# Hybrid decoder trunk: the instruction order made by the scheduler's timeline simulation instead of its core simulation

## The chip, the cores and the metric

The kernel runs on one core of a Trainium2 chip. The metric is the device time of one execution in microseconds (us), lower is better. The program is straight-line code: no loop is left at run time, and each engine carries out one fixed list of instructions.

## The reference

Four post-norm layers on a sequence of 1024 tokens with 1024 channels, all in float32. Layer i uses the token mixer i mod 3, so the order is short convolution, S5 state space, RWKV-7, short convolution.

```python
for i in range(DEPTH):
    kind, j = i % N_MIXERS, i // N_MIXERS
    if kind == 0:
        y = short_conv_mixer(x, conv_w_in[j], conv_k[j], conv_w_out[j])
    elif kind == 1:
        y = s5_mixer(x, ssm_w_in[j], ...)
    else:
        y = rwkv7_mixer(x, rwkv_mu[j], rwkv_w_rkvz[j], ...)
    r = DN_ALPHA * x + y
    r = r + (p[i] @ ple_proj[i]) * jax.nn.sigmoid(r @ ple_gate[i])
    x = layer_norm(r, ln_g[i], ln_b[i])
```

The convolution mixer has one 1024 x 4096 product, a convolution of width 3, gates and a 1024 x 1024 product. The S5 mixer has a 1024 x 2048 product, a diagonal complex scan and two 1024 x 1024 products. The RWKV mixer has four 1024 x 1024 products (r, k, v, z), two small low-rank products, a recurrence over the tokens with a 64 x 64 state in each of 16 heads, and a 1024 x 1024 product:

```python
def _rwkv_step(state, inp):
    r_t, w_t, k_t, v_t, kk_t, a_t = inp
    sa = jnp.einsum("bhvk,bhk->bhv", state, -kk_t)
    state = (state * w_t[:, :, None, :] + sa[..., None] * (kk_t * a_t)[:, :, None, :]
             + v_t[..., None] * k_t[:, :, None, :])
    out = jnp.einsum("bhvk,bhk->bhv", state, r_t)
    return state, out
```

## The kernel before

**Tiling.** Activations lie with channels on the 128 partitions: 8 blocks of channels (m = 0..7), and tokens in two halves of 512 (h = 0, 1). Every large product works with operands split into a high and a low part. `mm3` makes one 128 x 512 piece of a product with 24 matmuls of 512 columns: for each of 8 blocks of the contraction high times high (L308), high times low (L309) and low times high (L310). In what follows "a product" is such a piece of 24.

**Weights.** `wload` fetches one block of weights of 512 KB (L282, a DMA issued by SyncE, SP), casts it to its high part on ScalarE (`wh`, L285) and makes the low part on VectorE (`wl`, L286). Each of the three tiles has three buffers. `weight_order` lists the blocks in the order of use, and `wprep` starts the load two blocks ahead of use (`AHEAD = 2`).

**Background work.** Work that runs beside the products is written as Python generators. `pull` takes their next piece at fixed places between the products, by lists of small counts at the top of the S5 part (`CP`, `GP`, `UP`, `GR`, `IP`, `TP` and others). This sets the order in which instructions are traced. In conv layer 0 the tables of S5 are made that way, in the S5 layer the scan blocks, in the gate stages the layer norm of the half before (`ln_gen`).

**The RWKV layer.** For each half it computes z for the 8 blocks (with the low-rank parts), then v, then k and r block by block. A pair (m, h) is called a unit. For each unit `use_k` and `use_r` prepare the operands of the recurrence from the two products of k and r, `prep` makes the 64 x 64 score blocks, `tsolve` inverts unit triangular blocks on VectorE, `join` puts them together, and `seq` carries the state through 8 chunks of 64 tokens. One step of `seq`:

```python
nc.tensor.matmul(p1, R.ra[:, c, :], st, start=False, stop=False, skip_group_check=True)   # L1818
SC.copy(uv[rb, :], p1[rb, :])                                                          # L1819
p2 = sq("p2")
last = nc.tensor.matmul(p2[:, 0:P], R.kbt[c // 4][:, c % 4, :], uv, start=True, stop=True)  # L1822
for hd in range(2):
    V.scalar_tensor_tensor(st[cs, cs], st[cs, cs], R.pc[cs, c:c + 1], p2[cs, cs], ...)  # L1825
```

After the 8 steps come the output matmuls (L1832, 32 small ones), a group norm (L1846 and after), a scaling on GpSimd (L1853), a transposition on TensorE (`otp`, L1860) and a store. In `prep`, GpSimd scales `kb` (L1692), which TensorE then transposes (`kbtp`, L1697). The state goes to memory at the end of a unit of the first half (`dST`, L1837), and is fetched at the start of the same block in the second. At the turn from the first half to the second the layer reloads `x` of the second half from memory and builds the shifted operands of z from it (`xs3`).

**What sets the order.** The kernel names the engine of each operation, but not its place in the engine's list. The framework's scheduler makes the lists when the `TileContext` closes: it steps through a simulation of the core, and whenever an engine is free it gives it, out of the instructions that are ready, the one of the highest priority. Priority is the traced order, moved forward by `high_priority(offset=...)` for `tsolve` and `seq` (300) and `prep` and `join` (600). A few `issue_after` blocks forbid some moves. Buffers are handed out along the way. In the end the lists hold semaphore waits in place of the simulated times, so that on the chip each engine takes its list in order and waits at its head.

## Time and profile before

| what | value |
|---|---|
| median of 3 runs | 2874.41 us (2870.41 to 2875.98) |
| profiled execution | 2874.98 us, span 2873.3 us |
| instructions | 40597 |
| mean granted TensorE clock | 0.963 |
| busy share of TensorE (PE), its weight loads (PEld) | 95%, 75% |
| busy share of VectorE (DVE), ScalarE (ACT), GpSimd (POOL) | 66%, 39%, 22% |
| DMA | 312.67 MB, mean 109 GB/s |
| RWKV layer, from about 1150 to 2190 us | 1040 us |

The profile is one execution on the chip. Busy times are given for each engine; records of pipelined matmuls overlap, so a row of one matmul can read 0.40 us while the next starts 0.23 us later. In a table of windows each row is a stretch of the span. In a list of waits the row "A <- B" says that engine and instruction A stood idle until B ended, with the total, the number of times and the longest. L-numbers are lines of the kernel.

### The profile page before, as it was taken

The numbers are of one execution on the slowest core, as the hardware profiler recorded it, in microseconds if no ns is written. First come the engines' busy times: TensorE is split into PE (matmuls) and PEld (weight loads), VectorE is DVE, ScalarE is ACT, GpSimd is POOL, SyncE is SP. The second block draws the span as 40 slices with busy tenths as digits, with TensorE's granted clock in tenths as the row PEclk, the third lists the DMA queues.
The fourth block names the chain that finished last, engine by engine and source line by source line (L and its number), as shares of the span: only waits on it lengthen the run. The fifth ranks groups of instructions, "written<-read, shape, count | busy, mean of one in ns | idle before, by whom it ended". The sixth has DMA issues, their size and how long they took to land.

```text
span 2873.3 us, 40597 instructions
## 1 busy us (share of the span) xinstructions
PE 2722.6 (95%) x15131; PEld 2163.6 (75%) x15131; DVE 1886.0 (66%) x3428; ACT 1121.9 (39%) x2147; POOL 635.8 (22%) x690
## 2 busy tenths in 40 slices
PE   8999999999999999999888799898889999999998
PEld 6877788878877887577666577666667778888887
DVE  6787765477657347878788676887848473333654
ACT  3333322242144223655556465565534231112322
POOL 1243423221207033104333101333232210000000
PEclk9999999999999999999997799997899999999999
DMA  5333322358783333463222254222334332112320
GB/s 166 98 95 96 94 77 62 88 152 225 209 247 124 103 92 119 144 214 96 73 81 89 69 182 141 74 86 83 110 92 143 104 91 59 44 46 64 118 66 37
DMA packets 449749, 312.67 MB, mean 109 GB/s; under 512 B 48360, under 2 KB 393744, under 8 KB 449552
## 3 DMA queue, kind: packets, MB, share of 16 engines
q1 hardware_dynamic: 449552, 310.08, 36.0%
q8 instruction: 119, 1.95, 0.3%
q14 instruction: 78, 0.64, 0.1%
HBM read 240.28 MB, written 69.21 MB: 108 GB/s over the span
## 4 chain that ended last, share of the span: by engine, by line
PE 73%; DVE 14%; ACT 4%; issue 3%; POOL 2%; DMA 2%; SPq 0%; DVEq 0%; POOLq 0%; ACTq 0%
PE op L309 3%; PE op L308 3%; PE op L310 3%; PE gp L310 3%; PE zp L308 3%; PE gp L309 3%; PE zp L309 3%; PE zp L310 3%; PE gp L308 3%; PE sp L308 3%; PE sp L309 3%; PE sp L310 3%; DVE tv L1739 2%; PE hp L308 2%; PE hp L309 2%
## 5 line engine op out<-in xcount | busy, mean ns | idle before, releaser
L286 DVE TENSOR_TENSOR wl<-wraw,wh 128x1024 fp32r<-128x1024 f32 x283 | 365.9, 1294 | 311.5 <-ACT wh L285 303.5
L285 ACT CAST wh<-wraw 128x1024 fp32r<-128x1024 f32 x283 | 296.9, 1050 | 695.5 <-PE gp L309 191.8
L608 POOL TENSOR_TENSOR ln_s<-ln_s,rp 128x512 f32<-128x512 f32 x42 | 60.1, 1430 | 209.8 <-DVE rp L604 209.8
L1825 DVE SCALAR_TENSOR_TENSOR state<-state,pc,p 64x64 f32<-64x64 f32 x256 | 71.0, 277 | 50.1 <-PE p L1822 45.6
L1739 DVE TENSOR_TENSOR tv<-ti,mi 128x128 f32<-128x128 f32 (+3 forms) x128 | 97.1, 759 | 2.4
L1818 PE MATMUL p<-state,ra 128*128 128x128 f32 x256 | 65.7, 344 | 27.3 <-DVE state L1825 25.2
L1819 ACT COPY uv<-p 64x128 f32<-64x128 f32 x128 | 33.2, 259 | 138.8 <-PE p L1818 138.1
L1818 PEld LDWEIGHTS p<-state,ra 128*128 128x128 f32 x256 | 46.3, 219 | 52.7 <-DVE state L1825 42.1
L1673 PEld LDWEIGHTS s<-ra,kb 64*128 64x128 f32 x512 | 64.2, 212 | 20.4 <-ACT scr L1679 6.5
L1673 PE MATMUL s<-ra,kb 64*128 64x128 f32 x512 | 74.7, 314 | 4.4 <-ACT scr L1679 2.1
L1822 PE MATMUL p<-uv,kbt 128*128 128x128 f32 x256 | 67.7, 351 | 10.4 <-ACT uv L1819 10.3
L310 PE MATMUL gp<-r_0h,wl 128*128 128x512 f32 x192 | 76.9, 400 | 0.0
L308 PE MATMUL zp<-x_0h,wh 128*128 128x512 f32 x192 | 76.7, 400 | 0.0
L309 PE MATMUL gp<-r_0l,wh 128*128 128x512 f32 x192 | 76.7, 399 | 0.0
L308 PE MATMUL gp<-r_0h,wh 128*128 128x512 f32 x192 | 76.5, 398 | 0.0
L308 PE MATMUL gp<-r_1h,wh 128*128 128x512 f32 x192 | 76.4, 398 | 0.0
L310 PE MATMUL gp<-r_1h,wl 128*128 128x512 f32 x192 | 76.0, 396 | 0.1
L623 POOL TENSOR_TENSOR rp<-r_0h,r_0l 128x512 f32<-128x512 f32 x24 | 37.4, 1589 | 174.9 <-PE op L309 174.9
L308 PE MATMUL zp<-x_1h,wh 128*128 128x512 f32 x192 | 75.9, 396 | 0.0
L310 PE MATMUL zp<-x_1h,wl 128*128 128x512 f32 x192 | 75.8, 395 | 0.0
L309 PE MATMUL zp<-x_1l,wh 128*128 128x512 f32 x192 | 75.7, 394 | 0.0
L310 PE MATMUL zp<-x_0h,wl 128*128 128x512 f32 x192 | 75.7, 394 | 0.0
(740 smaller groups left out, 8437.6 us busy)
## 6 DMA issues: line engine op xcount, KB each, us to landing
wraw<-in_conv_w_in_dram SPq DMA_DIRECT2D x80, 512.0 KB
wraw<-in_rwkv_w_rkvz_dram SPq DMA_DIRECT2D x64, 512.0 KB
wraw<-in_ple_gate_dram SPq DMA_DIRECT2D x56, 512.0 KB
wraw<-in_conv_w_out_dram SPq DMA_DIRECT2D x24, 512.0 KB
wraw<-in_ssm_w_in_dram SPq DMA_DIRECT2D x21, 512.0 KB
xt<-xd SPq DMA_DIRECT2D x32, 256.0 KB
wraw<-in_rwkv_w_out_dram SPq DMA_DIRECT2D x16, 512.0 KB
wraw<-in_ple_proj_dram SPq DMA_DIRECT2D x14, 512.0 KB
```

The source lines that it names most:

```text
L285: nc.scalar.copy(wh, raw)
L286: nc.vector.tensor_tensor(wl, raw, f32(wh[:]), ALU.subtract)
L308: nc.tensor.matmul(ps, lh, xh, start=(k == 0), stop=False)
L309: nc.tensor.matmul(ps, lh, xl, start=False, stop=False)
L310: nc.tensor.matmul(ps, ll, xh, start=False, stop=(k == kt - 1))
L608: nc.gpsimd.tensor_tensor(s, s, rs, ALU.add)
L623: (eng or nc.gpsimd).tensor_tensor(rs, f32(rh[:]), f32(rl[:]), ALU.add)
L1673: nc.tensor.matmul(pss[hd][:, c * P:(c + 1) * P], kb[rows, 2 * c + w, :], ra[rows, 2 * c + w, :], start=True, stop=True)
L1739: V.tensor_tensor(tv, ti[:, b:8, 4 * b:4 * b + 4].unsqueeze(2).to_broadcast([P, n, c, 4]), mi[:, 4 * b:4 * b + 4, 0:c].rearrange("p q c -> ...
L1818: nc.tensor.matmul(p1, R.ra[:, c, :], st, start=False, stop=False, skip_group_check=True)
L1822: last = nc.tensor.matmul(p2[:, 0:P], R.kbt[c // 4][:, c % 4, :], uv, start=True, stop=True)
L1825: V.scalar_tensor_tensor(st[cs, cs], st[cs, cs], R.pc[cs, c:c + 1], p2[cs, cs], ALU.mult, ALU.add)
```

## The change

The scheduler steps through another simulation, the framework's timeline simulation. Both have costs for each instruction; they come from different models, in which engines, queues, transfers and semaphores are kept differently. The traced program, its priorities, its engines, its tiles and their buffer counts stay as they are.

```diff
-    with tile.TileContext(nc) as tc:
+    with tile.TileContext(nc, schedule_with_timeline_sim=True) as tc:
         body(tc, aps, out)
```

## The prediction

> **What bounds the kernel now.** I read the busy times first, then the clock, then the table of windows by layer, and last the matmuls and waits of the one layer that is left. Busy time on the page, and the clock from the view of the cores:

> ```profile
> PE 2722.6 (95%) x15131; PEld 2163.6 (75%) x15131; DVE 1886.0 (66%) x3428; ACT 1121.9 (39%) x2147; POOL 635.8 (22%) x690
> ...
> PE 73%; DVE 14%; ACT 4%; issue 3%; POOL 2%; DMA 2%; SPq 0%; DVEq 0%; POOLq 0%; ACTq 0%
> ```

> ```profile
> core 0: 2873.3 us, clock 0.963
> ```

> TensorE is busy for 95% of the span and carries 73% of the chain that ended last. An order cannot remove a matmul. It can only remove idle time of TensorE, 2873.3 - 2722.6 = 150.7 us, and time at a low clock. The windows (columns: length, busy time of PE, PEld, DVE, ACT and POOL with their counts, granted clock, DMA share, GB/s) say where both lie: before, in and after the RWKV layer.

> ```profile
> 0.00:1150.00 1150.00, 1120.84 (x5283) 904.37 (x5283) 753.66 (x1277) 369.37 (x539) 313.67 (x373) 1.00 0.44 128
> 1150.00:2190.00 1040.00, 932.58 (x6869) 713.99 (x6870) 796.99 (x1613) 570.44 (x1326) 265.46 (x264) 0.91 0.36 112
> 2190.00:2874.00 684.00, 669.22 (x2981) 545.25 (x2979) 335.38 (x540) 182.12 (x283) 56.70 (x54) 0.99 0.24 72
> ```

> Outside the RWKV layer TensorE idles 29.2 + 14.8 = 44 us in 1834 us, at a clock of 0.99 to 1.00. Inside it idles 1040 - 932.6 = 107.4 us, the clock is 0.91, and VectorE is busy for 797 us of 1040. So the order matters there.

> **What the change does there.** It adds no instruction, removes none and gives no engine other work. What moves is the place of each instruction in its engine's stream, and each engine takes its stream in that order. Within RWKV I follow one step of the recurrence, written in `seq`: a matmul of the state (L1818), a copy on ScalarE (L1819), a second matmul (L1822), two state updates on VectorE (L1825). There are 8 steps in each of 16 units (8 channel blocks, two halves), 128 in all. TensorE's stream in one step, with products of z from the turn between the halves beside it (start, duration, instruction):

> ```profile
> 1579.03 0.40 PE L1818 MATMUL p<-state,ra 128*128 128x128 f32 x2
> 1579.18 0.48 PE L310 MATMUL sp<-xs3h,wl 128*128 128x512 f32 x1
> 1579.50 0.40 PE L309 MATMUL sp<-xs3l,wh 128*128 128x512 f32 x1
> 1579.78 0.49 PE L1822 MATMUL p<-uv,kbt 128*128 128x128 f32 x2
> 1580.02 0.48 PE L310 MATMUL sp<-xs3h,wl 128*128 128x512 f32 x1
> 1580.33 0.39 PE L308 MATMUL sp<-xs3h,wh 128*128 128x512 f32 x1
> 1580.56 0.40 PE L309 MATMUL sp<-xs3l,wh 128*128 128x512 f32 x1
> 1580.79 0.39 PE L310 MATMUL sp<-xs3h,wl 128*128 128x512 f32 x1
> 1581.02 0.47 PE L1818 MATMUL p<-state,ra 128*128 128x128 f32 x2
> ```

> The step takes 1581.02 - 1579.03 = 1.99 us. While the chain is on ScalarE and VectorE, the order in place runs six large matmuls, which start 0.23 us apart (1580.33, 1580.56, 1580.79). Eight steps hold 48 of them, and 48 are two whole products of 24: as much as a unit has in its k and r stretch. What the order does is to lay these products into the gaps of the chain.

> The second measure is the time from unit to unit, by the last matmuls of each (L1832). First, last and the extreme pairs of the twelve ends that I use, six of each half of the sequence:

> ```profile
> 1420.57 1.15 PE L1832 MATMUL p<-uv,scr 128*64 128x64 f32 x32
> ...
> 1463.11 1.15 PE L1832 MATMUL p<-uv,scr 128*64 128x64 f32 x32
> ...
> 1509.00 1.15 PE L1832 MATMUL p<-uv,scr 128*64 128x64 f32 x32
> ...
> 1628.51 1.76 PE L1832 MATMUL p<-uv,scr 128*64 128x64 f32 x28
> ...
> 1851.64 1.15 PE L1832 MATMUL p<-uv,scr 128*64 128x64 f32 x32
> ...
> 1890.42 1.15 PE L1832 MATMUL p<-uv,scr 128*64 128x64 f32 x32
> ...
> 1927.03 1.15 PE L1832 MATMUL p<-uv,scr 128*64 128x64 f32 x32
> ...
> 2047.93 1.15 PE L1832 MATMUL p<-uv,scr 128*64 128x64 f32 x32
> ```

> The mean period is (1628.51 - 1420.57) / 5 = 41.6 us in the first half and (2047.93 - 1851.64) / 5 = 39.3 us in the second, 40.4 us over both. The longest is 1509.00 - 1463.11 = 45.9 us, the shortest 1927.03 - 1890.42 = 36.6 us. The recurrence work of a unit is the same each time. The spread, 3.8 us below the mean and 5.5 us above, is mostly what different orders of like work have cost in this kernel, and it bounds the change from both sides: 13 such periods (seven in each half, less the last, which runs out without products beside it) give 13 x -3.8 = -49 us and 13 x 5.5 = +71 us.

> **What an order can win.** The waits of TensorE in the layer (us in total, times, longest), then one of VectorE:

> ```profile
> PE p L1818 <- DVE state L1825: 25.2, 28, 2.8
> PE otp L1860 <- POOL o L1853: 14.1, 10, 6.8
> PE kbtp L1697 <- POOL kb L1692: 12.1, 11, 2.8
> PE p L1822 <- ACT uv L1819: 10.3, 24, 1.0
> ```

> ```profile
> DVE state L1825 <- PE p L1822: 45.6, 46, 2.9
> ```

> In each the head of a stream stood waiting, and what was behind it stood too. TensorE's four rows sum to 61.7 us. A simulation that foresees these latencies better puts other work in front. But VectorE, at 77% of the layer, needs those 45.6 us less than TensorE needs the chain: where a stall goes, the next thing late is the state update behind a weight split or a solve.

> **What an order can lose.** The gaps hold 16 x 48 x 0.23 = 177 us of products. An order that puts a unit's products in one block ahead of its chain leaves the gaps empty and pays them again in full. So the room is 61.7 us one way and 177 us the other. That asymmetry is why I put the forecast on the slower side, half way from the mean period to the longest: 13 x 2.7 = +35 us.

> **The other streams.** On SP every weight load (L282) stands in line with the stores of the recurrence:

> ```profile
> SPq L282 <- DVE state L1825: 50.9, 8, 14.9
> ```

> Eight loads stood behind a state up to 14.9 us. They cost nothing now because weights are fetched two blocks ahead (`AHEAD = 2`), which is 2 x 24 x 0.23 = 11 us of products. With that cover gone each would cost at most 14.9 - 11 = 4 us, 32 us for eight; I take nothing, since no weight row is among TensorE's largest waits, and leave it inside the range. GpSimd and ScalarE (265 and 570 us of 1040) have room; a GpSimd operation taken later shows up as the `otp` and `kbtp` rows above, 26 us, and at worst doubles them, which the +71 covers. Outside RWKV I take zero: TensorE has large products ready nearly all the time. Bounds there: -44 us, if all its idle time went, and +44 us, if it doubled, at the hand-overs between layers.

> **The sum.** The profiled execution took 2874.98 us, 1.7 around its span of 2873.3, and stands 0.6 above the median of the three runs (2874.41). 2874.98 + 35 = 2910 us.

> **The clock, and a rule.** Two stretches of 10 us show what small matmuls alone do:

> ```profile
> 1530.00:1540.00 10.00, 7.67 (x100) 5.92 (x104) 7.26 (x20) 2.64 (x8) 0.61 (x2) 0.50 0.55 173
> 2000.00:2010.00 10.00, 7.93 (x87) 6.23 (x83) 4.95 (x13) 3.65 (x8) 0.61 (x2) 0.50 0.01 3
> ```

> TensorE is busy for 77% and 79% there, so it cannot have idled more than 2.33 us at once, and yet the granted clock is 0.50. By these rows, an order that spreads large products into such stretches would lift the clock. All that it could give is 0.09 x 932.6 = 84 us. [...]

> **The rivals.**
> - Faster through better foresight: the new order fills the waits above and the units move half way to the shortest, 13 x -1.9 = -25 us: 2850 us. For it: 61.7 us of waits at the head of the stream, 46 waits of VectorE of 1 us each. Against: the six matmuls of a step already fill it. It decides once more than 35 of the 61.7 us are filled and the products stay in the gaps.
> - Faster through the clock as well: 25 us and half of the 84 us, -67 us: 2808 us. It needs products at the turn from the first half to the second, where they first need `x` reloaded.
> - Much slower: the scheduler picks TensorE's next instructions earlier than they can run, so that ready products of 24 go ahead of a chain step that is not ready yet. Half of a unit's products leave the gaps: 177 / 2 = +88 us, 2963 us; all of them +177 us, 3052 us. It decides against me once more than a fifth leave (35 of 177). Against it: later units have fewer ready products, so the block shrinks.
> - No difference: both simulations pick the same order where TensorE is the limit, or the flag does nothing. Then 2875 us. Against: the choice depends on time at every step, and one early difference shifts all that follows.

> **How the numbers follow.** Chances: longer units 0.37, much slower 0.14, better foresight 0.29, with the clock 0.07, no difference 0.13. So slower is 0.51, faster 0.36, and within 0.2% (5.7 us, about what three runs from 2870.41 to 2875.98 can tell apart) 0.13. The likeliest case by itself runs from 2881 to 2946 us. The range over the cases is 2822 to 2990 us: it holds the foresight case down to the shortest period (-49 us) and a little of the clock, and the blocked case up to 65% of the 177 us. About 0.07 is left out below and 0.08 above.

> **What would show it.** Right: nearly the same instruction counts, the windows outside RWKV within 10 us of now, the RWKV layer some 35 us longer, units 43 us apart instead of 40.4, more waits of L1818 for the state, TensorE's busy time about the same. Wrong towards faster: the four waits fall below 30 us and units come at 38 us. Wrong towards much slower: runs of 24 large matmuls with no L1818 between, and then chain steps with fewer than six. Wrong in place: if conv or S5 changes by over 20 us, the assumption that ready products cover everything outside RWKV has failed.

## Result: 9.3% slower

| | before | after |
|---|---|---|
| median of 4 runs each, one chip | 2875.19 us (2870.41 to 2881.53) | 3142.77 us (3135.47 to 3146.55) |
| ratio, 95% interval | | 1.0926 (1.0894 to 1.0958) |
| profiled span | 2873.3 us | 3144.8 us |
| TensorE busy / idle in the span | 2722.6 / 150.7 us | 2882.2 / 262.6 us |

The 271.5 us between the spans are two terms: TensorE idles 111.9 us longer, and the same 15131 matmul records occupy it 159.6 us longer. The second term is mostly the clock: 175 us of TensorE's busy time lay at half clock before and 478 us lie there after, and half of the 302 us between them is 151. First the busy times on the page and the mean granted clock of the kernel after, then its windows, cut at the same stages as the 1150 and 2190 us of before (columns as there):

```profile
PE 2882.2 (92%) x15131; PEld 2320.3 (74%) x15131; DVE 1908.2 (61%) x3428; ACT 1122.5 (36%) x2149; POOL 636.2 (20%) x690
```

```profile
core 0: 3144.8 us, clock 0.904
```

```profile
0.00:1175.00 1175.00, 1131.03 (x5283) 916.27 (x5283) 757.51 (x1271) 362.41 (x534) 317.74 (x369) 0.98 0.43 125
1175.00:2461.00 1286.00, 1087.08 (x6908) 863.61 (x6909) 816.15 (x1620) 579.91 (x1335) 262.11 (x270) 0.79 0.29 91
2461.00:3144.00 683.00, 664.04 (x2941) 540.38 (x2939) 334.48 (x538) 180.14 (x282) 56.31 (x54) 0.99 0.24 72
```

The RWKV layer grew from 1040 to 1286 us: 199 - 107 = 92 us of idle time and 1087.1 - 932.6 = 154.5 us of longer busy time. A granted clock of 0.79, made of stretches at 1.0 and at 0.5, means (1 - 0.79) / 0.5 x 1286 = 540 us at half clock; before it was (1 - 0.91) / 0.5 x 1040 = 187 us. The part ahead of it grew by 25 us. The part behind it took as long as before, but with 40 fewer matmul records in it (2941 against 2981), so some 9 us of the layer's growth are work that the new order put ahead of the cut.

Inside the layer, the last matmuls of the units (first and sixth of the first half; first, fifth and sixth of the second):

```profile
1471.98 1.98 PE L1832 MATMUL p<-uv,scr 128*64 128x64 f32 x32
...
1746.94 1.98 PE L1832 MATMUL p<-uv,scr 128*64 128x64 f32 x32
...
2046.21 1.98 PE L1832 MATMUL p<-uv,scr 128*64 128x64 f32 x32
...
2240.36 1.98 PE L1832 MATMUL p<-uv,scr 128*64 128x64 f32 x32
...
2322.45 1.15 PE L1832 MATMUL p<-uv,scr 128*64 128x64 f32 x32
```

A unit takes 55.0 us in the first half and 55.2 us in the second, where it took 41.6 and 39.3 (41.4 for the same five of the first half). The second mean is not of like work: the last of its five periods, 82.1 us, holds 198 large matmuls (almost all of the output product `op`) where it held 25 before. The four ahead of it take 48.5 us each, where they took 38.7. Part of a unit of the first half in TensorE's stream (start, duration, instruction, and in brackets the idle time before it and what ended it):

```profile
1573.84 0.38 PE L1818 MATMUL p<-state,ra 128*128 128x128 f32 x2
1574.16 1.16 PE L1673 MATMUL s<-ra,kb 64*128 64x128 f32 x8
1575.24 0.50 PE L310 MATMUL sp<-xs0h,wl 128*128 128x512 f32 x1
...
1576.97 0.38 PE L1822 MATMUL p<-uv,kbt 128*128 128x128 f32 x2
1579.15 0.49 PE L1818 MATMUL p<-state,ra 128*128 128x128 f32 x2 [1.80 <-DVE state L1825]
...
1581.16 0.49 PE L1818 MATMUL p<-state,ra 128*128 128x128 f32 x2 [0.69 <-DVE state L1825]
1582.00 0.49 PE L1822 MATMUL p<-uv,kbt 128*128 128x128 f32 x2 [0.35 <-ACT uv L1819]
1583.17 0.80 PE L1818 MATMUL p<-state,ra 128*128 128x128 f32 x2 [0.68 <-DVE state L1825]
...
1585.80 0.80 PE L1818 MATMUL p<-state,ra 128*128 128x128 f32 x2 [0.68 <-DVE state L1825]
1586.95 0.80 PE L1822 MATMUL p<-uv,kbt 128*128 128x128 f32 x2 [0.35 <-ACT uv L1819]
1587.67 1.98 PE L1832 MATMUL p<-uv,scr 128*64 128x64 f32 x32
1590.25 1.94 PE L1697 MATMUL kbtp<-ident,kb 128*128 128x128 f32 x8 [0.60 <-POOL state L1808]
...
1592.76 3.48 PE L1708 MATMUL wps<-uv,sca 64*64 64x64 f32 x32
1596.17 0.79 PE L308 MATMUL sp<-xs1h,wh 128*128 128x512 f32 x1
```

Three things are to be seen. L1822 at 1576.97 starts 3.13 us after its L1818, though further down 0.84 us is enough (1581.16 to 1582.00): eight L1673 and seven large matmuls stand between them. From 1579.15 on no product is left, and each step is a naked chain with 0.69 and 0.35 us of idle time. And between 1582.00 and 1583.17 the clock falls: the same matmuls go from 0.49 to 0.80 us and the step from 2.01 us (1579.15 to 1581.16) to 2.63 (1583.17 to 1585.80). The products come as a block, from 1596.17, its first matmuls at half clock. Count the large matmuls (L308 to L310) from one L1818 to the next, seven such steps in each of 16 units: of the 112 steps, 79 hold none; before it was 27.

The waits of TensorE (us in total, times, longest), and then the one of VectorE:

```profile
PE p L1818 <- DVE state L1825: 86.1, 69, 4.5
PE p L1822 <- ACT uv L1819: 22.3, 56, 1.3
PE pw L1363 <- ACT w L1361: 20.3, 11, 5.3
...
PE otp L1860 <- POOL o L1853: 7.9, 2, 7.0
...
PE up L308 <- ACT x_1h L191: 6.1, 1, 6.1
PE up L308 <- ACT x_0h L191: 5.4, 1, 5.4
```

```profile
DVE state L1825 <- PE p L1822: 112.7, 67, 5.0
```

### The profile page after: what moved, and what is told of

Same layout as the page of the kernel before. It is cut to its first block, busy times and chain, and to the rows that moved or that the text cites. A ratio compares the mean times of both kernels' runs of the same rounds, so it can differ in the third digit from the quotient of the medians.

```text
span 3144.8 us, 40665 instructions
## 1 busy us (share of the span) xinstructions
PE 2882.2 (92%) x15131; PEld 2320.3 (74%) x15131; DVE 1908.2 (61%) x3428; ACT 1122.5 (36%) x2149; POOL 636.2 (20%) x690
## 5 line engine op out<-in xcount | busy, mean ns | idle before, releaser
L1818 PE MATMUL p<-state,ra 128*128 128x128 f32 x256 | 81.1, 410 | 91.2 <-DVE state L1825 86.1
L1825 DVE SCALAR_TENSOR_TENSOR state<-state,pc,p 64x64 f32<-64x64 f32 x256 | 70.5, 275 | 116.6 <-PE p L1822 112.7
L1818 PEld LDWEIGHTS p<-state,ra 128*128 128x128 f32 x256 | 53.5, 255 | 115.2 <-DVE state L1825 103.2
L1822 PE MATMUL p<-uv,kbt 128*128 128x128 f32 x256 | 78.7, 401 | 22.5 <-ACT uv L1819 22.3
L1673 PEld LDWEIGHTS s<-ra,kb 64*128 64x128 f32 x512 | 81.5, 247 | 22.7 <-issue 9.0
L1673 PE MATMUL s<-ra,kb 64*128 64x128 f32 x512 | 95.4, 351 | 3.1 <-ACT scr L1679 1.4
L1819 ACT COPY uv<-p 64x128 f32<-64x128 f32 x128 | 33.1, 259 | 176.3 <-PE p L1818 175.7
L1739 DVE TENSOR_TENSOR tv<-ti,mi 128x128 f32<-128x128 f32 (+3 forms) x128 | 86.1, 672 | 4.6
L1822 PEld LDWEIGHTS p<-uv,kbt 128*128 128x128 f32 x256 | 55.0, 257 | 43.9 <-ACT uv L1819 37.8
L1677 DVE TENSOR_TENSOR sca<-s,mask 128x256 f32<-128x256 f32 x64 | 26.9, 421 | 96.1 <-PE s L1673 96.0
L308 PE MATMUL zp<-x_1h,wh 128*128 128x512 f32 x192 | 76.5, 398 | 1.0 <-ACT x_1h L191 1.0
L308 PE MATMUL gp<-r_0h,wh 128*128 128x512 f32 x192 | 77.3, 403 | 0.0
L309 PE MATMUL gp<-r_0l,wh 128*128 128x512 f32 x192 | 77.2, 402 | 0.0
L308 PE MATMUL zp<-x_0h,wh 128*128 128x512 f32 x192 | 77.0, 401 | 0.0
L310 PE MATMUL gp<-r_0h,wl 128*128 128x512 f32 x192 | 76.7, 399 | 0.0
L308 PE MATMUL gp<-r_1h,wh 128*128 128x512 f32 x192 | 76.0, 396 | 0.0
L310 PE MATMUL zp<-x_1h,wl 128*128 128x512 f32 x192 | 76.0, 396 | 0.0
L309 PE MATMUL gp<-r_1l,wh 128*128 128x512 f32 x192 | 75.9, 395 | 0.0
```

Source lines behind the costliest of these rows:

```text
L308: nc.tensor.matmul(ps, lh, xh, start=(k == 0), stop=False)
L309: nc.tensor.matmul(ps, lh, xl, start=False, stop=False)
L310: nc.tensor.matmul(ps, ll, xh, start=False, stop=(k == kt - 1))
L1673: nc.tensor.matmul(pss[hd][:, c * P:(c + 1) * P], kb[rows, 2 * c + w, :], ra[rows, 2 * c + w, :], start=True, stop=True)
L1739: V.tensor_tensor(tv, ti[:, b:8, 4 * b:4 * b + 4].unsqueeze(2).to_broadcast([P, n, c, 4]), mi[:, 4 * b:4 * b + 4, 0:c].rearrange("p q c -> ...
```

## Experiments

The framework's timeline simulation keeps a queue for each engine: instructions already chosen, their place in the list fixed, and not finished. Its length is a setting of that software, 35 for TensorE in the kernel after, and was not measured on the chip. Theory A was that this run-ahead makes the order: the choice is made so early that the next step of the recurrence is not ready, and a ready product is taken. Rivals were the simulation's other costs (B), the queues of the other engines (C), and priorities too small for it (D). Ratios are to the kernel before, on the same chip, with the 95% interval.

### The depth of the queue

The edit, with the depth N; nothing on the chip depends on it but the order:

```diff
+    from concourse import hw_specs as _hs
+    _hs.TRN2Spec.ENG_ISSUE_QUEUE_DEPTH = {**_hs.TRN2Spec.ENG_ISSUE_QUEUE_DEPTH, mybir.EngineType.PE: N}
     with tile.TileContext(nc, schedule_with_timeline_sim=True) as tc:
```

Depth 1:

> The timeline simulation gives each engine a queue of instructions that are chosen but not finished: 35 for TensorE, 12 for the others. Here TensorE's is set to 1, all else as in the kernel after. Theory A (run-ahead: TensorE's next instruction is chosen up to 35 ahead, when the next step of the recurrence is not ready yet, so ready products go in front of it): products return to the gaps, idle time before L1818 for the state falls from 91 us to under 40, mean clock rises from 0.904 to above 0.95, time 2840 to 2920 us. Theory B (the other costs of the timeline simulation, durations and DMA latencies, make the bad order): 3080 to 3160 us, clock about 0.90. Theory C (the queues of 12 of the other engines): no change, within 30 us of 3143.

3226.84 us, 1.1232 (1.1214 to 1.1250). Slower than any theory said. Its busy times and its largest wait:

```profile
PE 2831.7 (88%) x15131; PEld 2209.8 (69%) x15131; DVE 1874.0 (58%) x3428; ACT 1119.8 (35%) x2143; POOL 626.6 (19%) x690
```

```profile
PE p L1818 <- DVE state L1825: 110.3, 83, 7.9
```

The idle time is 3217.0 - 2831.7 = 385 us, and it grew in stages that hold no recurrence too (conv layer 0 from 613 to 641 us). By the count of steps above only 11 are empty, fewer than in any other version. So depth 1 spoils the order in a way of its own. That the simulation then takes TensorE for slower than it is, since no matmul overlaps the last, is argued and was not tried.

Depth 12:

> TensorE's queue at 12 instead of 35, all else as in the kernel after. Theory A: the damage is graded by the depth. In the list 66 of the 128 steps of the recurrence hold no large product, against 83 at 35, 30 in the kernel before and 11 at 1; by that, between the two kernels but nearer to after: 2990 to 3110 us. Theory B: within 30 us of 3143. A threshold (any depth beyond a step's six products does the whole harm): 3110 to 3160.

3023.28 us, 1.0527 (1.0503 to 1.0551): graded, as A expected.

Depth 4:

> TensorE's simulated queue at 4, all else as in the kernel after. Depth 12 gave 3023 us and depth 1 3227 us, so depth 1 has a cost of its own: the simulation then starts no matmul before the last has retired and takes TensorE to be slower than it is. Theory A (run-ahead does the harm, depth 1 is a second and separate error): 48 of the 128 steps hold no large product in the list, against 66 at 12; 2900 to 2990 us, clock above 0.93. Rival E (any other order of so many instructions is worse by a hundred us or two, the depth grades nothing): 3023 us or more.

2968.40 us, 1.0338 (1.0321 to 1.0356), inside A's range. Rival E, that any other order is worse and the depth grades nothing, stood for 3023 us or more.

Depth 2:

> TensorE's simulated queue at 2, all else as in the kernel after. So far 35, 12, 4 and 1 gave 3143, 3023, 2968 and 3227 us. In the list 45 of the 128 steps hold no large product (48 at 4) and 59 hold three to ten (37 at 4, 72 in the kernel before). Theory A (run-ahead does the harm, the error of depth 1 begins only where no matmul overlaps the last): 2890 to 2960 us. Rival H (the error of depth 1 is there at 2 already): above 2990 us.

2951.21 us, 1.0278 (1.0263 to 1.0293), inside A's range; H falls. The spans and clocks at 12, 4 and 2, one from each kernel:

```profile
core 0: 3020.5 us, clock 0.926
```

```profile
core 0: 2974.6 us, clock 0.931
```

```profile
core 0: 2944.6 us, clock 0.939
```

Steps without a large product, counted in the traces as above: 79 at 35, 61 at 12, 43 at 4, 41 at 2. Time and emptied steps fall together, and the clock rises. From 35 to 2, the depth of one queue is worth 3143 - 2951 = 192 of the 268 us.

### Everything but that depth

The queues of the four other engines at 1, TensorE's at 35:

```diff
+    _hs.TRN2Spec.ENG_ISSUE_QUEUE_DEPTH = {e: (v if e == mybir.EngineType.PE else 1) for e, v in _hs.TRN2Spec.ENG_ISSUE_QUEUE_DEPTH.items()}
```

> TensorE's queue stays at 35 and the queues of the four others are set to 1. Theory A (TensorE's run-ahead): within 40 us of 3143 us, clock 0.90, idle time before L1818 still 70 to 110 us. Theory C (VectorE and ScalarE run ahead and put ready work in front of the state updates): below 2980 us. Theory B (costs): within 40 us of 3143, as A; the first kernel of this job tells these two apart.

3140.03 us, 1.0939 (1.0921 to 1.0957): no change, C falls.

Priorities:

```diff
-PS, PT, PJ = 300, 300, 600
+PS, PT, PJ = 3000, 3000, 3000
```

> The kernel after with the priorities of prep, tsolve, join and seq moved forward by 3000 places instead of 300 and 600. Theory A: priority chooses only among what is ready at the time of choice; the next step of the recurrence is not, so it does not help: within 40 us of 3143 us, clock 0.89 to 0.92. Rival D (the offsets, chosen with the core simulation, are too small for the timeline simulation): below 3000 us.

3145.98 us, 1.0949 (1.0931 to 1.0968): no change, D falls. The reading is that a priority chooses among what is ready, and that the chain, 35 matmuls ahead, is not.

The simulation's write tails (its time from the end of an operation's stream until the result counts as written), set to nothing at depth 2 and at depth 35:

```diff
+    _hs.TRN2Spec.TIMELINE_SIM_WRITE_TAIL_CYCLES = {k: 0 for k in _hs.TRN2Spec.TIMELINE_SIM_WRITE_TAIL_CYCLES}
+    _hs.TRN2Spec.TIMELINE_SIM_ACTIVATE_EXTRA_TAIL_CYCLES = 0
+    _hs.TRN2Spec.PE_WRITE_TAIL_NS = 0.0
```

> TensorE's simulated queue at 2 and, in the simulation alone, no write tail behind the operations of VectorE, ScalarE and TensorE (results count as written when the stream ends). With the tails it took 2951 us. In the list 31 of the 128 steps hold no large product and 74 hold three to ten, as in the kernel before (30 and 72; with the tails 45 and 59). Theory A+B (depth does most, the longer links of the chain that the tails make do the rest): 2870 to 2930 us. Rival (the 80 us lie elsewhere, at the hand-over to S5 and in the recurrence's head): 2935 to 2975 us.

> The kernel after, its depths kept (35 and 12), without the write tails in the simulation. 82 of the 128 steps hold no large product in the list, 83 in the kernel after. Theory A (depth decides at 35): 3090 to 3160 us. Theory B (costs): below 3050 us.

At depth 2: 2922.82 us, 1.0178 (1.0159 to 1.0197), 28 us better than with the tails. At depth 35: 3154.27 us, 1.0976 (1.0957 to 1.0994), no better. So this cost matters once the depth is small, and not before. The simulation's other costs (durations, DMA latencies) were not varied. The simulation's own clock held at full, at depth 4:

```diff
+    import dataclasses as _dc
+    _hs.TRN2Spec.PE_CLOCK = _dc.replace(_hs.TRN2Spec.PE_CLOCK, entry_columns=0.0)
```

> TensorE's simulated queue at 4, and the simulation's own TensorE clock held at full (it models the lower clock, the core simulation does not model it in this way). What is left at depth 4 is 98 us over the kernel before. Theory B' (part of the rest is a price of the timeline simulation, here the slow clock by which it believes TensorE short of time): below 2940 us. Theory A alone (the rest is run-ahead of four): 2940 to 3000 us; in its list 56 steps hold no large product, 48 with the clock modelled, which speaks for this side.

2975.01 us, 1.0361 (1.0346 to 1.0376) against 1.0338: no gain. The last 50 us, from 2873 to the 2923 of depth 2 without tails, stay open: by stages, cut at the first matmuls of each, 15 us lie at the entry to S5, 15 us in z and v of the first half, 5 us in the last layer, the rest in the units.

### One wait by itself

In the z stage L1363, a small product, stands in front of the next large one and waits 20.3 us for a cast (L1361) whose inputs were there long ago: ScalarE does the sigmoid of the product just finished first (at 1223.67 us, for instance, and the cast at 1224.14). Of the eleven waits nine have clock 0.5 in them or within 1.8 us behind them; those of 1.6 us at 1822 and 0.4 us at 1861 have not. The cast was traced ahead of it:

```diff
     def use_z(m, h, ps, L, w2):
+        wt = T_("w2", [P, 4, P]).bitcast(F32R)
+        for i in range(2):
+            raw = w2[i][:, m * P:(m + 1) * P]
+            SC.copy(wt[:, i, :], raw)
+            V.tensor_tensor(wt[:, 2 + i, :], raw, f32(wt[:, i, :]), ALU.subtract)
         sg = T_("sg")
         SC.activation(sg, ps, AF.Sigmoid)
...
-        wt = T_("w2", [P, 4, P]).bitcast(F32R)
         for i, ps_ in enumerate((pw, pa)):
-            raw = w2[i][:, m * P:(m + 1) * P]
-            SC.copy(wt[:, i, :], raw)
-            V.tensor_tensor(wt[:, 2 + i, :], raw, f32(wt[:, i, :]), ALU.subtract)
```

> The kernel after with one edit: in use_z the casts of the low-rank weights (L1361, L1362) are traced ahead of the sigmoid of the product (L1352), so that ScalarE needn't finish the product's part before them. In the kernel after TensorE waits 20.3 us for that cast (15.8 and 4.5), in gaps up to 5.3 us, and each is followed by a stretch at clock 0.5. Theory A (in-order engines, a matmul taken early waits for a ScalarE queue that itself waits for the product before it; the lower clock doubles the price): 20 us of waits and 10 to 25 us of clock go, 3095 to 3125 us. Rival F (the wait moves to the next link, the sigmoid or the low part on VectorE): 3130 to 3155 us.

3116.55 us, 1.0856 (1.0828 to 1.0883), 26 us better. The stage from the entry to the layer to the first step of the recurrence (z and v of the first half), first in the kernel after, then with the cast ahead:

```profile
1175.00:1441.00 266.00, 222.21 (x1029) 164.46 (x1030) 176.03 (x289) 125.90 (x216) 37.17 (x42) 0.86 0.39 122
```

```profile
1171.00:1412.00 241.00, 212.61 (x1028) 159.20 (x1028) 178.01 (x293) 126.85 (x215) 38.50 (x42) 0.89 0.42 134
```

Idle time falls from 43.8 to 28.4 us, and TensorE's busy time falls by 9.6 us with it, at a clock of 0.89 in place of 0.86: here a gap is paid twice, once as idle time and once in the clock behind it.

### Is the clock a cause?

Three extra matmuls of 128 x 384 on constants were put into each step, results not read. First behind L1822, into the unused columns of its tile:

```diff
             last = nc.tensor.matmul(p2[:, 0:P], R.kbt[c // 4][:, c % 4, :], uv, start=True, stop=True)
+            with S.tc.issue_after(last.ins):
+                for _ in range(3):
+                    nc.tensor.matmul(p2[:, P:HT].rearrange("p (a b) -> p a b", b=P), S.rw.ones_r,
+                                     S.rw.ones_r[:].unsqueeze(1).to_broadcast([P, 3, P]), start=True, stop=True)
```

> The kernel after with three matmuls of 128 x 384 on constants after each L1822, into the unused columns of its tile; their results are not read. That is 384 more matmuls, 128 x 3 x 0.16 = 61 us of work at full clock (0.16 worked out from the 0.23 us of 512 columns), meant for the idle time of steps without products. Theory A (of the 270 us some 150 are the lower clock, which follows TensorE's own idling): the clock in the steps rises, mean clock above 0.93, 3010 to 3110 us. Rival G (the clock is a symptom only, idle waits set the time): 3143 plus 20 to 61 us, 3165 to 3205, clock within 0.01 of 0.904.

> The same three extra matmuls in each step of the kernel before, core simulation. There 83 us of the RWKV layer's TensorE time are lost to the lower clock, but most steps hold six products already, and the simulation knows nothing of the clock and plans the extra work as work. Theory A: the clock rises a little (0.963 to about 0.97), the extra 61 us of work take more than that gives back: 2875 to 2930 us. If the clock's share could be had this way, 2830 to 2865 us.

3233.80 us, 1.1267 (1.1238 to 1.1296), and 2949.03 us, 1.0272 (1.0257 to 1.0288). They lost 91 and 79 us against the kernels they were made from, more than the 61 us that the extra matmuls were estimated at (0.23 us for 512 columns makes 66 us; in the next run three of them take 0.61 us at full clock, 1525.68 to 1526.29, and 128 x 0.61 is 78 us), and both lie above every time that was expected. A step in the first (the edit shifts the lines: L1825 are the extra matmuls here, and L1829 is the state update):

```profile
1520.36 0.80 PE L1818 MATMUL p<-state,ra 128*128 128x128 f32 x2 [0.69 <-DVE state L1829]
1521.50 0.80 PE L1822 MATMUL p<-uv,kbt 128*128 128x128 f32 x2 [0.35 <-ACT uv L1819]
1521.95 1.31 PE L1825 MATMUL p<-c_ones_r 128*128 128x384 f32 x3
1523.95 0.80 PE L1818 MATMUL p<-state,ra 128*128 128x128 f32 x2 [0.69 <-DVE state L1829]
```

```profile
1523.30 0.59 DVE L1829 SCALAR_TENSOR_TENSOR state<-state,pc,p 64x64 f32<-64x64 f32 x2 [3.00 <-PE p L1825]
```

The state update begins behind the extra matmuls (L1825), not behind L1822: it waited for all that writes the tile, and the step takes 3.59 us. This test says nothing about the clock. Put between L1818 and L1822, where only ScalarE is waited for:

```diff
-            nc.tensor.matmul(p1, R.ra[:, c, :], st, start=False, stop=False, skip_group_check=True)
+            first = nc.tensor.matmul(p1, R.ra[:, c, :], st, start=False, stop=False, skip_group_check=True)
...
             p2 = sq("p2")
-            last = nc.tensor.matmul(p2[:, 0:P], R.kbt[c // 4][:, c % 4, :], uv, start=True, stop=True)
+            with ExitStack() as q:
+                q.enter_context(S.tc.issue_after(first.ins))
+                for _ in range(3):
+                    wm = nc.tensor.matmul(p2[:, P:HT].rearrange("p (a b) -> p a b", b=P), S.rw.ones_r,
+                                          S.rw.ones_r[:].unsqueeze(1).to_broadcast([P, 3, P]), start=True, stop=True)
+                    q.enter_context(S.tc.issue_after(wm.ins))
+                last = nc.tensor.matmul(p2[:, 0:P], R.kbt[c // 4][:, c % 4, :], uv, start=True, stop=True)
```

> The kernel after with the three extra matmuls of 128 x 384 (results not read) moved ahead of L1822, into the time of ScalarE's copy: in the earlier try they stood behind L1822 in its tile, VectorE waited for them, and a step without products took 3.59 us in place of 2.6. Counted from the rows of the kernels before and after, the clock rose only after a stretch of 3.41 us with at least 3,072 full-height columns (all 68 rises) and fell after fewer (69 of 70 falls below 3,500). A step without products has 1,024 in 2.0 us, 1,750 in 3.41 us; with the extra 1,152 it has 3,700 and should hold the full clock once it has it. Theory A (the lower clock is a cause): mean clock above 0.925, steps of 2.0 to 2.2 us, 3040 to 3120 us. Rival G (a symptom only): clock 0.90, 3150 to 3210 us.

3156.69 us, 1.0986 (1.0960 to 1.1012), mean clock 0.923. Each theory was right in one half: the clock rose almost to A's 0.925, the time did not fall, as G said. The time at half clock went from 609 to 489 us and gave back some 59 us (busy 2901.2, less 78 for the extra matmuls at 0.61 us for three at full clock, against 2882.2); the extra work took that and more. Two of its steps, one at full and one at half clock (L1825 are the extra matmuls, L1828 the second matmul of the step, L1831 the state update):

```profile
1525.44 0.49 PE L1818 MATMUL p<-state,ra 128*128 128x128 f32 x2 [1.97 <-DVE state L1831]
1525.68 0.77 PE L1825 MATMUL p<-c_ones_r 128*128 128x384 f32 x3
1526.29 0.47 PE L1828 MATMUL p<-uv,kbt 128*128 128x128 f32 x2
1527.45 0.80 PE L1818 MATMUL p<-state,ra 128*128 128x128 f32 x2 [0.69 <-DVE state L1831]
...
1530.32 0.80 PE L1818 MATMUL p<-state,ra 128*128 128x128 f32 x2 [0.69 <-DVE state L1831]
```

At full clock the step with them takes 2.01 us, as without. At half clock it takes 2.87 instead of 2.63 and stays there: one late state (1.97 us) came ahead of the loss of the clock, and the filling is too thin to win it back by the count of columns in the last section (2,176 columns in 2.87 us, some 2,590 in 3.41 us). In the kernel before, in 32 steps only:

> The kernel before (core simulation) with the same three extra matmuls ahead of L1822, in the steps of four units only: blocks 4, 6 and 7 of the first half and block 4 of the second, whose steps hold few products or none; 32 steps. Some 139 us at clock 0.5 lie in those stretches. Theory A: about 25 steps go from 2.6 to 2.0 us, 15 us, and some matmuls after them run at full clock: 2835 to 2862 us, clock above 0.970. Rival G, or a list that shifts by as much as is won: 2865 to 2900 us.

2869.89 us, 1.0001 (0.9991 to 1.0010), mean clock 0.970 where it was 0.963. Again the clock rose and the time stood. So no run shows that a clock bought with extra work shortens the kernel; that the lower clock is part of the price rests on the busy times of the same records. No version here beats the kernel before.

## Why the prediction was wrong

- **What bounds the kernel, and what stays the same:** right. Records and busy times of the other engines hardly moved, and the place is the RWKV layer.
- **The mechanism** was among the rivals, as "much slower": ready products of 24 go ahead of a chain step that is not ready. It had 0.14. Its signature was there in the main: 12 of the 112 steps hold 24 large matmuls or more, where none did, and in eight units the 24 of a product lie in two neighbouring steps (20 and 4, for instance), with the other five empty. What stood against it, that later units have fewer ready products, failed as to the block: the first four units of the second half are emptied like those of the first, though a unit there loses less time (48.5 against 38.7 us).
- **The term of the sum, 13 x 2.7 = +35 us**, is the step that failed first. I took the spread of the units in the kernel before, 36.6 to 45.9 us, as the bounds of what another order can cost. All those units were ordered by one rule of choice. Their spread bounds the luck within that rule, not another rule: over those nine of the ten periods that hold like work the mean is 52.1 us where it was 40.2, 13 x 11.9 = 155 us.
- **A stage without a term.** The sum gave nothing to the stage ahead of the first step, z and v of the first half. It grew from 200 to 266 us, with 33 more matmul records in it; its row before (the row after stands above, from 1175 to 1441 us):

```profile
1150.00:1350.00 200.00, 187.01 (x996) 138.64 (x996) 164.50 (x273) 123.26 (x213) 36.79 (x37) 0.97 0.50 157
```

- **The clock** is the step that failed next, and it put even the worst case, 3052 us, below the result. I priced it as something to win (84 us) and nowhere as something to lose. The layer's idle time grew by 92 us, inside that rival's 88 to 177; its longer busy time, most of it the lower clock, added 154.5 us, in no case of mine. "TensorE's busy time about the same" was therefore wrong by 160 us.
- **Outside RWKV, zero:** wrong by 25 us, and by the mark I had set, "S5 changes by over 20 us". At this hand-over between layers, too, ready products (the gate of the second half, `gp`) went ahead of a chain, the layer norm of the first half. Its last transposition on TensorE, before and after:

```profile
596.72 1.05 PE L692 MATMUL ln_y<-ident,ln_r 128*128 128x128 f32 x8
```

```profile
601.79 1.05 PE L692 MATMUL ln_y<-ident,ln_r 128*128 128x128 f32 x8
```

  It comes 5.1 us later, and the first product of S5 then waits 5.4 us for `x_0h`, the next half's 6.1 us for `x_1h` (the two `up` rows above). The operand of the transposition was ready at 597.64 us, 4.1 us ahead of it. VectorE's list adds to it: behind this transposition it does all eight L697 in one block (4.87 us from 602.88) before the first L705, where in the kernel before the two are mixed, and the first cast of `x_0h` starts at 608.24 us, where it started at 599.92.
- **Better foresight** was right on two rows of four: the waits for GpSimd fell from 14.1 to 7.9 us (`otp`) and from 12.1 to 0.4 us (`kbtp`). The two rows of the recurrence rose from 35.5 to 108.4 us.
- **SP and the weights, zero:** right. L282 behind a state fell from 8 to 3 times, and no wait of TensorE for a weight cast exceeds 1.6 us.

## To carry to other kernels

Ask of a list scheduler when it fixes an instruction's place, not only how well it knows durations: if it chooses a queue's length ahead, work that is always ready passes the chain, and here neither priorities nor shorter write tails brought it back at depth 35. A shorter queue is not always better: depth 1 was the worst. Price the clock on both sides of every change of order on TensorE: here the order with the emptied steps had 111.9 us more idle time and, by an estimate from the clock records, some 151 us from half clock besides. Spread within one kernel's order bounds only orders made by the same rule.

## What the runs showed of the hardware

```profile
1462.99:1466.40 3.41, 1.69 (x8) 1.12 (x8) 2.07 (x4) 0.52 (x2) 0.00 (x0) 1.00 0.14 38
1466.40:1469.81 3.41, 1.99 (x6) 1.11 (x5) 0.88 (x4) 0.26 (x1) 0.00 (x0) 0.50 0.41 120
...
1476.64:1480.05 3.41, 3.41 (x33) 3.39 (x33) 2.04 (x4) 3.22 (x19) 2.12 (x4) 0.50 0.00 2
1480.05:1483.47 3.42, 3.42 (x12) 2.72 (x11) 3.28 (x13) 0.58 (x1) 1.20 (x1) 0.50 0.00 0
1483.47:1486.88 3.41, 3.41 (x45) 2.56 (x44) 3.13 (x9) 0.00 (x0) 0.00 (x0) 1.00 0.00 0
```

In these rows the work of a window goes with the clock of the next. After 1.69 us of work, with no gap inside the window longer than 0.69 us (another, of 2.03 us, ends 0.34 us into it), the clock falls. After 3.41 us that are busy throughout, mostly with the 64 x 64 matmuls of L1708, it does not rise; after a window of large matmuls it does. So idle time alone does not account for these rows, and a count of columns through the array does. In the count that follows a large matmul and an L1818 or L1822 have 512 each (a large one holds TensorE for 0.23 us at full and 0.43 us at half clock, an L1818 for 0.24 and 0.45 us by the rows at 1525.44 and 1527.45 above), small matmuls are counted roughly, and a matmul of half the rows counts half. Counted in full, the window at 1476.64 would have some 3,750, and 77 of the 167 windows of before and after behind which half clock stayed would have more than 2,990; counted half, it has 1,880, and 25 of the 167 have more. In the traces of all sixteen kernels, the 608 rises all follow a window of some 2,990 columns or more, and nine in ten of the 624 falls follow one of 2,990 or fewer. About 3,000 is thus an estimate of the threshold in these runs. It does not account for all: of 1,467 windows after which half clock stayed, 206 count more. At half clock 3,000 is three quarters of what a window can hold (eight 512-column matmuls at 0.43 us), at full clock less than half (3.41 us at 0.23 us each hold some 7,600). A naked step at half clock has 1,024 columns in 2.63 us, some 1,330 in a window, so by this estimate a chain that loses the clock does not win it back by itself; the longest stretch at half clock in the kernel after lasts 89 us, from 2183 to 2272 us, over a unit whose steps hold no large matmul.
